# Token norms in a mixture of experts: gathered beside one expert, normed beside the next, in two fused vector passes

## The chip, the cores and the metric

One core of one Trainium2 chip runs the whole program. A core has TensorE (PE, matrix products), VectorE (DVE), ScalarE (ACT), GpSimd (POOL) and SyncE (SP), each with an in-order queue of its own, and 16 DMA engines that they share. The metric is device time of one execution in microseconds (us); lower is better.

## The reference

A decoder layer with 2048 tokens of 1024 values: a mixer, a LayerNorm, a mixture of 16 experts with two experts for a token, and a second LayerNorm. The change lies in the second half:

```python
def moe(x, ...):                       # idx, w = route(x): 2 of 16 experts a token
    ...
    h = jax.nn.silu(xb @ w_gate[e]) * (xb @ w_up[e])      # w_gate, w_up: 1024 x 512
    return h @ w_down[e]                                   # w_down: 512 x 1024
...
x = layer_norm(ALPHA * x + moe(x, ...), ln2_g[l], ln2_b[l])

def layer_norm(x, g, b):
    mu = jnp.mean(x); var = jnp.mean(jnp.square(x - mu))   # over a token's 1024 values
    return (x - mu) * lax.rsqrt(var + LN_EPS) * g + b
```

## The kernel before

The function `moe_phase` treats the experts in 16 steps, s = 0 to 15, in an order chosen on the chip. A step has room for CAPS[s] tokens: 264 in steps 8 and 9, 256 from step 10 on (two chunks of 128 rows). A product in float32 is made of three passes over high and low halves, so every operand is split on the chip: ScalarE copies the high half, VectorE subtracts to get the low half.

**The first product** of a step (`gemm1`, line 62, tiles `ph`) has four quarters j. A quarter takes two weight tiles, gate and up, of 128x1024; each is loaded by SyncE into `raw` (four buffers), copied by ScalarE (L1569) and completed by VectorE (L1570, tile `w`, four buffers). When both results are there, ScalarE applies silu (L1575) and VectorE multiplies (L1576, tile `sl`); that product of the activations is what the change hangs the norms on. ScalarE and VectorE then split it into `h` (L1584, L1585). After quarters 1 and 2 the halves of the down weights are split as well (L1546, L1547, 128x2048).

**The second product** (`gemm2`, L1621, tiles `py`) multiplies `h` with the down weights. For a chunk of 128 rows, TensorE first takes the quarters 0 to 2 of both halves and then quarter 3. ScalarE evicts to `z` (L1636, two buffers), and GpSimd adds it to the sum `zd` in DRAM by an indirect scatter (L1658). Between these products TensorE transposes the next step's tokens (L1484), whose halves go to `xt` (L1486). TensorE's order is written by hand; the other engines' orders come from a scheduler that goes by a simulated time line.

**The next steps' tokens** come by `fetch`: SyncE loads the slot table (`tab`, L1461), VectorE makes indices of it (`tb`, `ig`, `io`, L1463 to L1467), and GpSimd gathers the rows (`xg`, L1471). SyncE issues the table's load behind the weight loads, each of which stands for a `raw` buffer that a split on VectorE releases.

**The norm of finished tokens.** The tokens are put into an order (`fin`) by the last of their experts, and after step s - 1 a known number of blocks of 128 tokens is final (READY). Beside step s the function `tokens` norms those blocks: 2, 1, 2, 1, 2, 2, 2 and 4 in steps 8 to 15. For each, GpSimd gathers the rows from `zd` (`zt`, L1524), VectorE takes the statistics of the two halves (L1527), aggregates them (L1501) and adds epsilon (L1503), GpSimd raises to -1/2 (L1504), VectorE computes the shift (L1506), ScalarE scales and shifts (L1509), GpSimd multiplies with g (L1510), VectorE adds b (L1511), and GpSimd scatters the result to the output (L1532). The gather can't be issued before the last scatter of step s - 1 has landed in `zd`. Tiles `zt` and `o` have two buffers.

The last step's own 256 tokens are added to a gathered residual and normed in `gemm2` itself (L1633 to L1663, L1514, L1515). A loop for overflowing slots and one for tokens whose norm must be repeated follow; they run zero times here.

Of the kernel before, what the change touches and what calls it, by code (L numbers as in the profile page):

```python
# [11 lines left out]
F32 = mybir.dt.float32  # L12
# [5 lines left out]
OP = mybir.AluOpType  # L18
# [4 lines left out]
D = 1024  # L23
# [5 lines left out]
ALPHA = 2.0 ** 0.25  # L29
# [988 lines left out]
NE = 16  # L1018
# [408 lines left out]
def moe_phase(c):  # L1427
    nc, tc, a = c.nc, c.tc, c.a
    v = nc.vector
    CM = CAPS[0]  # L1430
    NCH = (CM + 127) // 128
    with ExitStack() as es:
# [20 lines left out]
        def indirect(idx):  # L1453
            return bass.IndirectOffsetOnAxis(ap=idx, axis=0)
# [60 lines left out]
                v.scalar_tensor_tensor(o[:r, vs], o[:r, vs], rs[:r], b2[:r, vs], op0=OP.mult, op1=OP.add)  # L1515
            return o

        def tokens(row=None, idx=None):

            z = yp.tile([128, D], F32, name="zt")  # L1520
            if idx is None:
                nc.gpsimd.dma_start(z, c.z[ds(row, 128), :])
            else:
                nc.gpsimd.indirect_dma_start(out=z, out_offset=None, in_=c.z[:, :], in_offset=indirect(idx))  # L1524
            st = sm.tile([128, 2, 6], F32, name="st")
            for hf in range(2):
                v.bn_stats(st[:, hf], z[:, hf * 512:(hf + 1) * 512])  # L1527
            o = normed(z, st, 128)
            if idx is None:
                nc.gpsimd.dma_start(out[ds(row, 128), :], o)  # L1530
            else:
                nc.gpsimd.indirect_dma_start(out=out, out_offset=indirect(idx), in_=o, in_offset=None)  # L1532

        def after(order, *instructions):
            for i in instructions:
                order.enter_context(tc.issue_after(i.ins))
# [13 lines left out]
        def gemm1(f, e, C, first=False, late=False):  # L1550
            xh = lambda k: f["xt"][k // 4][:, 0, k % 4]
            xl = lambda k: f["xt"][k // 4][:, 1, k % 4]
            h = ht[:, :, :C], ht[:, :, 384:384 + C]

            off = stacked(C)
            full = C // 128 * 128 if off else C
            for j in range(4):
                ps = []
                for w in (wg, wu):
                    raw = w1p.tile([128, KC, 128], F32, name="raw1")  # L1560
                    load = nc.sync.dma_start(raw, w[ds(e, 1), :, j * 128:(j + 1) * 128].rearrange("o (k p) f -> p (o k) f", p=128))
                    if j == 1 and first:

                        hold(c, load, f["gather"])
                    t = w1p.tile([128, 2, KC, 128], F32R, name="w1")
                    with ExitStack() as order:
                        if j and first:
                            after(order, *f["last"])
                        nc.scalar.activation(t[:, 0], raw, AF.Copy)  # L1569
                        v.tensor_tensor(out=t[:, 1], in0=raw, in1=f32(t[:, 0]), op=OP.subtract)  # L1570
                    pg = ps_h.tile([128, 512], F32, name="ph")[:, :C]
                    matmul3(nc, pg, lambda k: t[:, 0, k], lambda k: t[:, 1, k], xh, xl, KC)
                    ps.append(pg)
                sl = hp.tile([128, CM], F32, name="sl", bufs=2)[:, :C]
                silu = nc.scalar.activation(sl, ps[0], AF.Silu)  # L1575
                mul = v.tensor_tensor(out=sl, in0=sl, in1=ps[1], op=OP.mult)  # L1576
                f.setdefault("mul", mul)

                with ExitStack() as order:
                    after(order, silu, mul)  # L1580
                    for part in THEN[j]:
                        if part < 2:
                            f["w"] = f.get("w", []) + [down(e, part)]
                nc.scalar.activation(h[0][:, j], sl, AF.Copy)  # L1584
                low = v.tensor_tensor(out=h[1][:, j, :full], in0=sl[:, :full], in1=f32(h[0][:, j, :full]), op=OP.subtract)  # L1585
                if off:
                    v.tensor_tensor(out=ht[:, j, full + off:C + off], in0=sl[:, full:], in1=f32(h[0][:, j, full:]), op=OP.subtract)
                if 2 in THEN[j] and late:
                    with ExitStack() as order:
                        after(order, low)  # L1590
                        residual(f, C)
            f["h"] = h
# [91 lines left out]
        with tc.manual_schedule(engines={mybir.EngineType.PE}):  # L1684
            r = plan_slots(c, pl, ps_y)

            big = lambda n: yp.tile([128, D], F32, name="zt")[:, :n * NE].rearrange("p (n e) -> p n e", e=NE)
            order_, over = plan_order(c, pl, ps_y, r, big), plan_over(c, pl, r, big)
            f = start(0)
            early = sm.tile([128, 128], BF16, name="early")  # L1690
# [2 lines left out]
            for step in transposes(f, CAPS[0]):  # L1693
                step()
                keep_warm(c, ps_y, WARM5)
            for s in range(NE):
                late = last = s == NE - 1
                nxt = start(s + 1) if 0 < s < NE - 1 else None
                gemm1(f, E[s], CAPS[s], s == 0, late)
                with ExitStack() as order:  # L1700
# [5 lines left out]
                    else:  # L1706
# [2 lines left out]
                            next(over, None)  # L1709
                        for _ in range(0 if s < 3 else 2 if s == 5 else 1):  # L1710
                            next(order_, None)
                for b in range(READY[s - 2] if s > 1 else 0, READY[s - 1] if s else 0):

                    tokens(idx=c.fin[:, b, 0:1])
                work = gemm2(f, E[s], CAPS[s], late, last)
                if nxt:
                    steps = transposes(nxt, CAPS[s + 1])
# [12 lines left out]
            run(gemm2(f, e, 128))  # L1730
        n = nc.values_load(c.nagain[0:1, 0:1], min_val=0, max_val=S // 128)
        with tc.For_i(0, n, 1) as i:
            tokens(row=i * 128)


def fill_tables(c, pad, part):
# [53 lines left out]
```

## Time and profile before

| | |
|---|---|
| Time, median of 3 runs | 1772.26 us (1771.97 to 1775.58) |
| The profiled execution's own time | 1779.3 us |
| Its span, first to last instruction | 1777.8 us |
| Mean granted TensorE clock | 0.941 |
| TensorE busy | 1546.0 us, 87% |
| VectorE busy | 1200.3 us, 68% |
| ScalarE busy | 773.7 us, 44% |
| GpSimd busy | 641.2 us, 36% |
| DMA | 260.77 MB, mean 147 GB/s |
| First products of steps 8 to 15 begin at | 1341.83, 1405.78, 1454.07, 1504.33, 1552.33, 1600.41, 1649.20 and 1694.70 us |

The shares are means over phases with different limits: the mixer ends near 950 us, and the steps 8 to 15, the ones with norms, take the last 436 us. For these the list of waits and the engines' timelines say more than the shares. In such rows a name such as `zt<-zd,fin` reads "tile zt, made from zd and fin", L1527 is line 1527 of the kernel before, and a wait is put down to the event that ended it.

### The profile page before, as it was taken

Reading aid. Unit: us, or ns where it says so; the run is one execution under the profiler, and the core shown is the slowest. Engines: PE = TensorE matmul, PEld = TensorE weight load, DVE = VectorE, ACT = ScalarE, POOL = GpSimd, SP = SyncE. Lnnn points to the kernel's source line nnn. Section 1 sums busy time; section 2 is a strip of 40 time slices with the busy share of each in tenths; the row PEclk is TensorE's granted clock in tenths of the full one; section 3 lists DMA queues with packets and bytes.
Section 4 is the critical chain, followed back from the end, with each engine's and each line's share of the span. In section 5 each row is a group of like instructions: output and inputs, shape, how many; then the busy total and the mean of one; then the engine's idle time right before and its main releaser. Section 6 shows DMA issues by size and latency. Waiting matters only on the chain. (4 is left out here: it accounts for less than half of the span.)

```text
span 1777.8 us, 28720 instructions
## 1 busy us (share of the span) xinstructions
PE 1546.0 (87%) x10277; PEld 1383.0 (78%) x10277; DVE 1200.3 (68%) x2900; ACT 773.7 (44%) x1605; POOL 641.2 (36%) x814
## 2 busy tenths in 40 slices
PE   8899999888889988889995999999995986877881
PEld 7899999877888887767773999988884876777770
DVE  5788888985888888578885566555542555565643
ACT  4567676762211123233322545555543453444430
POOL 3233343555555544123232221111233424233334
PEclk9999999999999999989997999999998998988895
DMA  9422222432123213444324987777674866778642
GB/s 274 127 90 90 90 90 90 149 102 79 55 63 97 63 42 95 162 154 172 125 96 138 308 209 198 196 193 192 180 186 101 225 191 195 206 210 234 182 118 100
DMA packets 241166, 260.77 MB, mean 147 GB/s; under 512 B 25301, under 2 KB 190358, under 8 KB 241020
## 3 DMA queue, kind: packets, MB, share of 16 engines
q1 hardware_dynamic: 213680, 182.11, 33.5%
q0 software_dynamic: 22224, 71.84, 15.4%
q10 hardware_dynamic: 5116, 4.94, 0.9%
q8 instruction: 83, 1.36, 0.3%
q14 instruction: 63, 0.52, 0.1%
HBM read 189.97 MB, written 70.60 MB: 147 GB/s over the span
## 5 line engine op out<-in xcount | busy, mean ns | idle before, releaser
L62 PE MATMUL ph<-xt,w 128*128 128x256 f32 (+8 forms) x3072 | 416.1, 298 | 80.9 <-DVE w L1570 76.2
L62 PEld LDWEIGHTS ph<-xt,w 128*128 128x128 f32 x3072 | 412.3, 196 | 86.0 <-DVE w L1570 78.5
L62 PE MATMUL pj<-xt,w 128*128 128x256 f32 x2016 | 294.7, 291 | 11.4 <-DVE xt L138 3.9
L62 PEld LDWEIGHTS pj<-xt,w 128*128 128x128 f32 x2016 | 264.3, 194 | 17.1 <-DVE xt L138 5.4
L1621 PE MATMUL py<-w,h 128*128 128x512 f32 (+8 forms) x936 | 244.6, 407 | 3.8 <-ACT z L1636 2.0
L1570 DVE TENSOR_TENSOR w<-raw,w 128x1024 fp32r<-128x1024 f32 x128 | 161.0, 1272 | 69.3 <-ACT w L1569 68.9
L1621 PEld LDWEIGHTS py<-w,h 128*128 128x128 f32 (+8 forms) x936 | 160.6, 180 | 50.0 <-issue 3.4
L62 PE MATMUL py<-w,xt 128*128 128x512 f32 x672 | 172.4, 405 | 0.0
L1569 ACT ACTIVATE w<-raw 128x1024 fp32r<-128x1024 f32 x128 | 132.7, 1053 | 59.8 <-PE ph L62 41.6
L1658 POOL DMA_INDIRECT zd<-z,io x40 | 69.7, 1743 | 236.5 <-ACT xt L1486 140.0
L62 PEld LDWEIGHTS py<-w,xt 128*128 128x128 f32 x672 | 122.8, 191 | 27.1 <-issue 4.6
L1486 DVE TENSOR_TENSOR xt<-tr,xt 128x512 fp32r<-128x512 f32 (+8 forms) x84 | 49.4, 595 | 69.2 <-ACT xt L1486 69.1
L62 PE MATMUL pj<-w,xt 128*128 128x512 f32 x336 | 88.4, 402 | 0.0
L338 POOL TENSOR_SCALAR prob<-prob,den 128x128 f32<-128x128 f32 x128 | 46.2, 380 | 108.3 <-ACT prob L381 57.8
L793 DVE TENSOR_TENSOR qb<-qq,F 64x256 f32<-64x256 f32 x112 | 83.5, 745 | 2.0
L1471 POOL DMA_INDIRECT xg<-x1d,ig x42 | 45.4, 1080 | 86.8 <-issue 33.9
L1547 DVE TENSOR_TENSOR w<-raw,w 128x2048 fp32r<-128x2048 f32 x32 | 75.2, 2350 | 0.7 <-ACT w L1546 0.7
L1527 DVE BATCH_NORM_STATS2 st<-zt 128x6 f32<-128x512 f32 x32 | 20.5, 681 | 80.1 <-DMA zt<-zd,fin 80.1
L1235 POOL DMA_INDIRECT T<-row,dst x32 | 34.5, 1077 | 111.0 <-DVE dst L1233 92.2
L811 DVE COPY_PREDICATED A<-mask,pl 128x512 f32<-128x512 uint8 x56 | 50.0, 893 | 32.1 <-PE pl L809 31.1
L1486 ACT ACTIVATE xt<-tr 128x512 fp32r<-128x512 f32 (+8 forms) x84 | 43.7, 521 | 62.0 <-PE tr L1484 62.0
L1636 ACT ACTIVATE z<-py,tb 128x512 f32<-128x512 f32 (+1 forms) x62 | 42.6, 688 | 62.3 <-PE py L1621 60.8
(366 smaller groups left out, 2937.3 us busy)
## 6 DMA issues: line engine op xcount, KB each, us to landing
raw<-in_w_gate SPq DMA_DIRECT2D x64, 512.0 KB, 6.9
raw<-in_w_up SPq DMA_DIRECT2D x64, 512.0 KB, 6.6
raw<-in_w_down SPq DMA_DIRECT2D x32, 1024.0 KB, 8.5
xd<-xt SPq DMA_DIRECT2D x32, 512.0 KB, 6.6
xr<-in_x SPq DMA_DIRECT2D x14, 1024.0 KB, 6.3
xt<-xd POOLq DMA_DIRECT2D x20, 512.0 KB, 5.0
raw<-mixT SPq DMA_DIRECT2D x16, 512.0 KB, 4.6
x1d<-x SPq DMA_DIRECT2D x16, 512.0 KB, 2.6
```

Source lines behind the costliest of these rows:

```text
L62: nc.tensor.matmul(ps, lhsT=a, rhs=b, start=i == 0, stop=i == len(steps) - 1)
L338: nc.gpsimd.tensor_scalar(prob[:, h], prob[:, h], den[:, h:h + 1], 1.0, op0=OP.mult, op1=OP.mult)
L793: nc.vector.tensor_tensor(out=qb[l][rw, :, :, o].rearrange("p a c (n i) -> p (a c) n i", i=h), in0=sec(Qv), in1=sec(Fv), op=OP.mult)
L811: c.level = nc.vector.copy_predicated(A.rearrange("p c h (n u i) -> p (c h n) u i", u=2, i=h)[:, :, 1], mask[:, l].rearrange("p m (n i) -> ...
L1471: gather = nc.gpsimd.indirect_dma_start(out=X[:r, n], out_offset=None, in_=c.x1[:, :], in_offset=indirect(ig[:r, n:n + 1]))
L1486: f["last"] = nc.scalar.activation(hi, pt, AF.Copy), v.tensor_tensor(out=lo, in0=pt, in1=f32(hi), op=OP.subtract)
L1547: v.tensor_tensor(out=t[:, 1], in0=raw, in1=f32(t[:, 0]), op=OP.subtract)
L1569: nc.scalar.activation(t[:, 0], raw, AF.Copy)
L1570: v.tensor_tensor(out=t[:, 1], in0=raw, in1=f32(t[:, 0]), op=OP.subtract)
L1621: nc.tensor.matmul(pys[hf][:m], lhsT=lhs, rhs=rhs, start=k == 0 and i == 0, stop=k == 3 and i == len(steps[k]) - 1)
L1636: nc.scalar.activation(z[:r, hs], py[:r], AF.Copy, scale=weight)
L1658: nc.gpsimd.indirect_dma_start(out=c.z[:, :], out_offset=at, in_=z[:r], in_offset=None, bounds_check=S - 1, oob_is_err=False, compute_op=O ...
```

## The change

`tokens` is cut into three parts. `bring` gathers a block; `scale` takes the statistics and the power; `write` norms in two fused VectorE passes (subtract the mean and multiply with g; multiply with the power and add b) and scatters the result. A block brought beside step s is normed beside step s + 1. `zt` gets a third buffer. The two parts of a norm are ordered behind the products of the activations (`f["muls"]`, one a quarter): `scale` of the n-th block behind quarter n's, `write` behind quarter n + 1's, at most 3. In the last step the four blocks that are left are brought and normed too, behind the last quarters.

```diff
-        def tokens(row=None, idx=None):
+        def bring(row=None, idx=None):
-            z = yp.tile([128, D], F32, name="zt")
+            z = yp.tile([128, D], F32, name="zt", bufs=3)
...
+            return dict(z=z, row=row, idx=idx)
+        def scale(t):
             st = sm.tile([128, 2, 6], F32, name="st")
             for hf in range(2):
-                v.bn_stats(st[:, hf], z[:, hf * 512:(hf + 1) * 512])
-            o = normed(z, st, 128)
...
+                v.bn_stats(st[:, hf], t["z"][:, hf * 512:(hf + 1) * 512])
+            t["mv"] = sm.tile([128, 2], F32, name="mv")
+            v.bn_aggr(t["mv"], st)
+            t["rs"] = sm.tile([128, 1], F32, name="rs")
+            v.tensor_scalar(t["rs"], t["mv"][:, 1:2], 1e-5 / ALPHA ** 2, None, op0=OP.add)
+            nc.gpsimd.tensor_tensor(out=t["rs"], in0=t["rs"], in1=mh, op=OP.pow)
+        def write(t):
+            o = yp.tile([128, D], F32, name="o")
+            v.scalar_tensor_tensor(o, t["z"], t["mv"][:, 0:1], g2, op0=OP.subtract, op1=OP.mult)
+            v.scalar_tensor_tensor(o, o, t["rs"], b2, op0=OP.mult, op1=OP.add)
...
                 f.setdefault("mul", mul)
+                f["muls"] = f.get("muls", []) + [mul]
...
-                for b in range(READY[s - 2] if s > 1 else 0, READY[s - 1] if s else 0):
-                    tokens(idx=c.fin[:, b, 0:1])
+                def norm(n, t):
+                    for k, part in enumerate((scale, write)):
+                        with ExitStack() as order:
+                            after(order, f["muls"][min(n + k, 3)])
+                            part(t)
+                ids = [c.fin[:, b, 0:1] for b in range(READY[s - 2] if s > 1 else 0, READY[s - 1] if s else 0)]
+                for n, t in enumerate(brought):
+                    norm(n, t)
+                brought = [bring(idx=i) for i in ids[:3]]
+                if last:
+                    for n in range(len(ids)):
+                        norm(2 + n // 2, brought[n])
+                        if n + 3 < len(ids):
+                            brought.append(bring(idx=ids[n + 3]))
```

TensorE's and SyncE's orders are the same in both kernels, apart from line numbers. On VectorE, step 14, from the first quarter's product on, before (`sl` is that product, `w` of 128x1024 a split of the first product's weights, `w` of 128x2048 one of the down weights):

```order
L1576 TENSOR_TENSOR sl<-sl,ph 128x256
L1570 TENSOR_TENSOR w_17895<-raw_17893,w_17895 128x1024
L1585 TENSOR_TENSOR h<-sl,h 128x256
L1527 BN_STATS st<-zt 128x6 x2
L1501 BN_AGGR mv<-st 128x2
L1503 TENSOR_SCALAR rs<-mv 128x1
L1506 SCALAR_TENSOR_TENSOR nm<-mv,rs 128x1
L1527 BN_STATS st<-zt 128x6 x2
L1576 TENSOR_TENSOR sl<-sl,ph 128x256
L1547 TENSOR_TENSOR w_17858<-raw_17856,w_17858 128x2048
L1570 TENSOR_TENSOR w_17935<-raw_17933,w_17935 128x1024
```

The same place in the changed kernel, up to the splits of the fourth quarter:

```order
L1590 TENSOR_TENSOR sl<-sl,ph 128x256
L1531 BN_STATS st<-zt 128x6 x2
L1584 TENSOR_TENSOR w_17841<-raw_17839,w_17841 128x1024
L1600 TENSOR_TENSOR h<-sl,h 128x256
L1533 BN_AGGR mv<-st 128x2
L1535 TENSOR_SCALAR rs<-mv 128x1
L1590 TENSOR_TENSOR sl<-sl,ph 128x256
L1561 TENSOR_TENSOR w_17804<-raw_17802,w_17804 128x2048
L1541 SCALAR_TENSOR_TENSOR o<-zt,mv,g_11350 128x1024
L1531 BN_STATS st<-zt 128x6 x2
L1584 TENSOR_TENSOR w_17881<-raw_17879,w_17881 128x1024
L1584 TENSOR_TENSOR w_17911<-raw_17909,w_17911 128x1024
```

The statistics stood for blocks gathered in the same step; now they are of blocks gathered a step before, and a fused pass and the second block's statistics stand ahead of the fourth quarter's splits. The rows go on as follows, up to the third quarter's low half `h`, which the second product reads:

```order
L1600 TENSOR_TENSOR h<-sl,h 128x256
L1542 SCALAR_TENSOR_TENSOR o<-o,rs,b_11351 128x1024
L1533 BN_AGGR mv<-st 128x2
L1590 TENSOR_TENSOR sl<-sl,ph 128x256
L1561 TENSOR_TENSOR w_17874<-raw_17872,w_17874 128x2048
L1584 TENSOR_TENSOR w_18070<-raw_18068,w_18070 128x1024
L1584 TENSOR_TENSOR w_18100<-raw_18098,w_18100 128x1024
L1535 TENSOR_SCALAR rs<-mv 128x1
L1541 SCALAR_TENSOR_TENSOR o<-zt,mv,g_11350 128x1024
L1584 TENSOR_TENSOR w_18135<-raw_18133,w_18135 128x1024
L1600 TENSOR_TENSOR h<-sl,h 128x256
```

Three fused passes in all stand between the second quarter's product and that half. The second place is VectorE at the end of step 11, where the slot table of a later step (`tab`) is read between the low halves `xt` of step 12's tokens. Before:

```order
L1486 TENSOR_TENSOR xt_16769<-tr,xt_16769 128x4x128
L1486 TENSOR_TENSOR xt_16770<-tr,xt_16770 128x4x128 x2
L1463 TENSOR_TENSOR tb<-tab 128x4
L1465 TENSOR_SCALAR ig<-tb 128x2
L1467 CAST io<-tb 128x2
L1570 TENSOR_TENSOR w_17023<-raw_17021,w_17023 128x1024
```

And in the changed kernel:

```order
L1486 TENSOR_TENSOR xt_16739<-tr,xt_16739 128x4x128 x2
L1463 TENSOR_TENSOR tb<-tab 128x4
L1465 TENSOR_SCALAR ig<-tb 128x2
L1467 CAST io<-tb 128x2
L1486 TENSOR_TENSOR xt_16740<-tr,xt_16740 128x4x128 x2
L1584 TENSOR_TENSOR w_16993<-raw_16991,w_16993 128x1024
```

Two of the four low halves now stand behind the table; in the changed kernel it is two in step 9 and one in steps 10 and 12; before, it was one in each of these. The third place is GpSimd, from the gathers of step 14's blocks on. Before:

```order
L1524 DMA zt_17998<-zd_88,fin_14987 128x1024
L1524 DMA zt_18015<-zd_88,fin_14987 128x1024
L1504 TENSOR_TENSOR rs_18005<-rs_18005,mh_11355 128x1
L1510 TENSOR_TENSOR o_18010<-o_18010,g2_11350 128x1024
L1532 DMA out_0<-o_18010,fin_14987 2048x1024
L1504 TENSOR_TENSOR rs_18022<-rs_18022,mh_11355 128x1
L1510 TENSOR_TENSOR o_18027<-o_18027,g2_11350 128x1024
L1532 DMA out_0<-o_18027,fin_14987 2048x1024
L1658 DMA zd_88<-z_18034,io_17302 2048x1024
```

And in the changed kernel:

```order
L1524 DMA zt_17968<-zd_88,fin_14987 128x1024
L1536 TENSOR_TENSOR rs_17949<-rs_17949,mh_11355 128x1
L1524 DMA zt_17970<-zd_88,fin_14987 128x1024
L1546 DMA out_0<-o_17952,fin_14987 2048x1024
L1536 TENSOR_TENSOR rs_17961<-rs_17961,mh_11355 128x1
L1546 DMA out_0<-o_17964,fin_14987 2048x1024
L1673 DMA zd_88<-z_17974,io_17254 2048x1024
```

The multiplies with g are gone, the power and the output scatter are of blocks gathered a step earlier and stand behind the first new gather, and the second gather stands behind the first power.

More of the change, by code (lines that the diff above doesn't have):

```diff
@@ L1524, in tokens @@
                 nc.gpsimd.indirect_dma_start(out=z, out_offset=None, in_=c.z[:, :], in_offset=indirect(idx))
+            return dict(z=z, row=row, idx=idx)
+        def scale(t):
             st = sm.tile([128, 2, 6], F32, name="st")
             for hf in range(2):
-                v.bn_stats(st[:, hf], z[:, hf * 512:(hf + 1) * 512])
-            o = normed(z, st, 128)
-            if idx is None:
-                nc.gpsimd.dma_start(out[ds(row, 128), :], o)
+                v.bn_stats(st[:, hf], t["z"][:, hf * 512:(hf + 1) * 512])
[8 more added lines that the diff above has]
+            v.scalar_tensor_tensor(o, o, t["rs"], b2, op0=OP.mult, op1=OP.add)
+            if t["idx"] is None:
+                nc.gpsimd.dma_start(out[ds(t["row"], 128), :], o)
             else:
-                nc.gpsimd.indirect_dma_start(out=out, out_offset=indirect(idx), in_=o, in_offset=None)
+                nc.gpsimd.indirect_dma_start(out=out, out_offset=indirect(t["idx"]), in_=o, in_offset=None)
         def after(order, *instructions):
@@ L1685, in moe_phase @@
             r = plan_slots(c, pl, ps_y)
-            big = lambda n: yp.tile([128, D], F32, name="zt")[:, :n * NE].rearrange("p (n e) -> p n e", e=NE)
+            big = lambda n: yp.tile([128, D], F32, name="zt", bufs=3)[:, :n * NE].rearrange("p (n e) -> p n e", e=NE)
             order_, over = plan_order(c, pl, ps_y, r, big), plan_over(c, pl, r, big)
@@ L1695, in moe_phase @@
                 keep_warm(c, ps_y, WARM5)
+            brought = []
             for s in range(NE):
@@ L1732, in moe_phase @@
         with tc.For_i(0, n, 1) as i:
-            tokens(row=i * 128)
+            t = bring(row=i * 128)
+            scale(t)
+            write(t)
 def fill_tables(c, pad, part):
```

## The prediction

> **What bounds the kernel now.** I read the list of waits first, because the engine shares (PE busy 87% of the span) say nothing about one stage. Columns: engine, line waited at, releaser, then total us, times, longest.
>
> ```profile
> DVE st L1527 <- DMA zt<-zd,fin: 80.1, 9, 13.3
> PE ph L62 <- DVE w L1570: 76.2, 10, 17.0
> DVE tb L1463 <- DMA tab<-T: 72.2, 14, 7.9
> POOL zt L1524 <- DMA zd<-z,io: 37.6, 7, 7.8
> ```
>
> The first two have nearly the same size: VectorE stands 80.1 us before the statistics of a gathered token block, and TensorE stands 76.2 us for weight splits that VectorE makes. The timeline of VectorE in step 10 shows that the two are one stall (start, duration, engine, line, operation; in brackets the idle time ahead and its releaser):
>
> ```profile
> 1463.59 0.41 DVE L1585 TENSOR_TENSOR h<-sl,h 128x256 fp32r<-128x256 f32 x1
> 1475.52 1.29 DVE L1527 BATCH_NORM_STATS2 st<-zt 128x6 f32<-128x512 f32 x2 [11.51 <-DMA zt<-zd,fin]
> ...
> 1478.01 0.42 DVE L1576 TENSOR_TENSOR sl<-sl,ph 128x256 f32<-128x256 f32 x1
> ```
>
> VectorE is in order: 11.51 us before the statistics, and the splits for the last quarter of the first product stand behind them. TensorE's timeline has this once in each of the steps 8 to 15:
>
> ```profile
> 1379.73 8.65 PE L62 MATMUL ph<-xt,w 128*128 128x264 f32 x46 [17.00 <-DVE w L1570]
> 1430.22 7.43 PE L62 MATMUL ph<-xt,w 128*128 128x264 f32 x46 [6.59 <-DVE w L1570]
> 1483.97 7.63 PE L62 MATMUL ph<-xt,w 128*128 128x256 f32 x46 [11.78 <-DVE w L1570]
> 1532.13 7.47 PE L62 MATMUL ph<-xt,w 128*128 128x256 f32 x46 [6.64 <-DVE w L1570]
> 1552.33 17.43 PE L62 MATMUL ph<-xt,w 128*128 128x256 f32 x146
> 1580.47 7.22 PE L62 MATMUL ph<-xt,w 128*128 128x256 f32 x46 [10.72 <-DVE w L1570]
> 1600.41 17.43 PE L62 MATMUL ph<-xt,w 128*128 128x256 f32 x146
> 1624.68 7.30 PE L62 MATMUL ph<-xt,w 128*128 128x256 f32 x46 [6.84 <-DVE w L1570]
> 1673.78 8.19 PE L62 MATMUL ph<-xt,w 128*128 128x256 f32 x46 [7.18 <-DVE w L1570]
> 1694.70 17.43 PE L62 MATMUL ph<-xt,w 128*128 128x256 f32 x146
> 1720.08 7.36 PE L62 MATMUL ph<-xt,w 128*128 128x256 f32 x46 [7.95 <-DVE w L1570]
> ```
>
> The eight waits are 17.00 + 6.59 + 11.78 + 6.64 + 10.72 + 6.84 + 7.18 + 7.95 = 74.7 us. TensorE is what the rest of these steps waits for, so they lie on the path.
>
> **The change, part by part.**
>
> *The wait goes.* A block is gathered beside one step and read beside the next, over 20 us later, while a gather lands 4.2 to 6.3 us after its issue:
>
> ```profile
> DMA to landing us min/median/max: 4.2/5.1/6.3
> ```
>
> No statistics then wait for their gather in steps 9 to 14. TensorE's and SyncE's orders stay as they are. On GpSimd the power and the output scatters now stand behind the new gathers, and the second gather of steps 13 to 15 stands for a buffer that a fused pass releases; behind these are a step's own scatters, which come half a step later. **Gain 74.7 us.**
>
> *The slow matmuls behind each wait go.* At full speed 146 matmuls of 256 columns take 17.43 us, 0.1194 each, so 46 take 5.49, and 5.66 with 264 columns (steps 8 and 9). The 46 behind the waits took 8.65, 7.43, 7.63, 7.47, 7.22, 7.30, 8.19 and 7.36: together 17.0 us more. The granted clock agrees: in the busy times by stretch (last three numbers of a row: granted clock, DMA share, GB/s; the first with an x is TensorE) it is 1.00 in step 1, where TensorE never waits, and 0.86 in step 10.
>
> ```profile
> 1026.00:1072.00 46.00, 46.00 (x283) 41.95 (x282) 28.62 (x51) 22.58 (x31) 11.88 (x9) 1.00 0.78 196
> 1454.00:1504.00 50.00, 37.76 (x256) 35.10 (x256) 26.95 (x39) 22.80 (x30) 20.51 (x13) 0.86 0.69 197
> 1600.00:1649.00 49.00, 40.02 (x259) 36.14 (x258) 27.27 (x38) 21.33 (x28) 17.95 (x13) 0.90 0.80 221
> ```
>
> A short wait costs clock too. In step 13, TensorE stood 2.02 us and the next 12 matmuls took 4.61 us, against 3.04 for 12 a moment later: 1.6 more.
>
> ```profile
> 1641.53 4.61 PE L1621 MATMUL py<-w,h 128*128 128x512 f32 x12 [2.02 <-ACT z L1636]
> ...
> 1646.32 3.04 PE L1621 MATMUL py<-w,h 128*128 128x512 f32 x12
> ```
>
> I therefore add 1.6 us to every new wait of some 2 us or more. The Trainium skill (TensorE: Matmul & The Clock Gate, What's actually happening) says that the clock falls only after an idle window of about 3.4 us. By that rule the new waits below would cost no clock, and the sum would be some 10 us better; the row of 2.02 us speaks against it.
>
> **Gain 17.0 us.** The 2.02 us wait itself is for an evicted block whose scatter came late, because GpSimd was busy with the norms' multiplies and output scatters; those multiplies go: **gain 3.6 us**, nothing if the scatter stays late.
>
> *What VectorE gets.* The norm leaves ScalarE (one activation) and GpSimd (one multiply per block), and VectorE's one add becomes two fused passes. Nothing waits for ScalarE or GpSimd here except the chain removed above, so I count no gain for them. A fused pass of 832 columns takes 1.085 us; for 1024 I take 1.25 from start to start, between that and its length scaled by columns (1.34).
>
> ```profile
> L1514 DVE SCALAR_TENSOR_TENSOR o<-z,mv,g x2: 1085/1085/1085, 1753.3 to 1762.3; 128x832 f32<-128x832 f32 x2
> ```
>
> For the rest, start to start, from step 9: product 0.34, down weights' split 2.20, two splits 2.27, low half 0.34.
>
> ```profile
> 1432.77 0.42 DVE L1576 TENSOR_TENSOR sl<-sl,ph 128x264 f32<-128x264 f32 x1
> 1433.11 2.28 DVE L1547 TENSOR_TENSOR w<-raw,w 128x2048 fp32r<-128x2048 f32 x1
> 1435.31 2.35 DVE L1570 TENSOR_TENSOR w<-raw,w 128x1024 fp32r<-128x1024 f32 x2
> 1437.58 0.41 DVE L1585 TENSOR_TENSOR h<-sl,h 128x256 fp32r<-128x256 f32 x1
> ```
>
> A first product lasts 192 x 0.1194 = 22.9 us, a quarter 5.73. By the fixed order, VectorE does the following from the second quarter's product (at 11.6) to the third quarter's low half, with two blocks: 0.34 + 2.20 + pass 1.25 + statistics 1.3 + 2.27 + 0.34 + pass 1.25 + aggregate 0.2 + 0.34 + 2.20 + 2.27 + add 0.1 + pass 1.25 + split 1.14 + 0.34 = 16.8, so it ends at 28.4. The second product needs that half after 8 matmuls of 0.25, at 22.9 + 2.05 = 24.95: 3.4 us late. With one block the list is 2.85 shorter: 0.6 late. Two blocks are normed beside steps 9, 11, 13 and 14, one beside 10 and 12. **Loss 4 x (3.4 + 1.6) + 2 x 0.6 = 21.2 us.** Bounds: 0, if TensorE's own small waits give the room, and twice that.
>
> *The table wait comes to the front.* VectorE also stands for the slot table, in its order among the transposes' low halves. The table landed 12.5 and 10.4 us after the end of the split that releases its issue (steps 10 and 12):
>
> ```profile
> 1493.19 1.22 DVE L1570 TENSOR_TENSOR w<-raw,w 128x1024 fp32r<-128x1024 f32 x1
> 1506.85 0.16 DVE L1463 TENSOR_TENSOR tb<-tab 128x4 f32<-128x4 f32 x1 [6.02 <-DMA tab<-T]
> 1507.23 0.68 DVE L1486 TENSOR_TENSOR xt<-tr,xt 128x512 fp32r<-128x512 f32 x1
> ...
> 1588.82 1.23 DVE L1570 TENSOR_TENSOR w<-raw,w 128x1024 fp32r<-128x1024 f32 x1
> 1600.42 0.16 DVE L1463 TENSOR_TENSOR tb<-tab 128x4 f32<-128x4 f32 x1 [2.05 <-DMA tab<-T]
> ```
>
> By the list, that split ends at 27.0 with one block and 29.9 with two; the table then is there at 38.5 and 41.4, and the low halves behind it take 1.0 (one) or 1.65 (two). TensorE needs them 1.4 us into the next step. A step without waits is 1600.41 - 1552.33 - 10.72 - 1.73 = 35.6 us, so the need is at 37.6 with one block and at 42.0 with two. New waits: step 10 to 11 and 12 to 13 1.9 each (one low half behind the table; + 1.6 each), 11 to 12 1.0 (two behind it): 8.0 us. Of these, 3.5 are there now, at the start of step 11 (1.95 and 1.6 of clock):
>
> ```profile
> 1507.97 17.52 PE L62 MATMUL ph<-xt,w 128*128 128x256 f32 x133 [1.95 <-DVE xt L1486]
> ```
>
> **Loss 4.5 us**, bounds 0 and 11.
>
> *The last step.* TensorE's first product now ends at 1720.08 + 7.36 = 1727.4, and from there to the end of the span (1777.8) are 50.4 us; VectorE starts the last step's own norm here:
>
> ```profile
> 1753.35 1.08 DVE L1514 SCALAR_TENSOR_TENSOR o<-z,mv,g 128x832 f32<-128x832 f32 x1 [3.48 <-DMA out<-o,fin]
> ```
>
> Behind it VectorE will have nine passes (11.3), two pairs of statistics (2.6), four evictions (2.8), their statistics (2.5), small ones (1.2) and the pass at L1514 (1.1), 21.5 in all, with some 3 us of waits for the last two gathers, whose buffers come free late; from L1514 on, 24.5 us remain as now. That is 49 instead of 50.4: **gain 1.4 us**, bounds -6 and +6.
>
> **The sum.** 74.7 + 17.0 + 3.6 - 21.2 - 4.5 + 1.4 = 71.0 us. The profiled execution took 1779.3 us, so 1708.3. It lies 7.0 us above the median of the runs, 1772.26; I carry that over: **1701 us**.
>
> **The rivals.**
>
> *Nothing new waits.* The losses of 21.2 and 4.5 do not come: 1701 - 26 = 1675. For it: in step 1 TensorE was busy 46.00 of 46.00 us, with 28.6 us of VectorE beside it. Against it: 16.8 us of VectorE work in 13.4. Chance 0.12.
>
> *The clock holds through waits of 2 to 3 us.* Six additions of 1.6 fall away: 1701 - 10 = 1691. This is what the Trainium skill's page on the clock gate would give. Against it stands the row of 2.02 us. Chance 0.15.
>
> *The transfers bind.* In step 13 the DMA engines were busy 0.80 of 49 us, 39 us of work; the others have about 35 (step 10: 0.69 of 50). My steps 8 to 14 sum to about 290 us, 41 each, a share of 0.85. The highest share at which TensorE never waited is 0.78 (1026 to 1072). If that is the limit, a step takes 35/0.78 = 45 us, seven of them 314: 24 more, 1725, and up to 1745 if the weights come in an order that starves the splits. Against it: in bursts the engines are busy throughout. Chance 0.22.
>
> *Slower.* GpSimd raises the variance to the power -1/2 behind the new gathers in its queue, and these stand until the last scatter has landed:
>
> ```profile
> 1472.44 0.97 POOL L1524 DMA_INDIRECT zt<-zd,fin  x1 [0.30 <-issue]
> ```
>
> Step 10 began at 1454.1, so the gathers were out at 19.3 us; the second pass asks for the power at about 20 (11.6 + the list to there). Each us later stops VectorE, all splits and TensorE behind it, in seven steps. It eats the 71 us when the gathers come 10 us later than now, and ends at 1772 + 91 - 71 = 1792 when they come 13 later. Nothing in the trace moves them so far; GpSimd gets less to do. Chance 0.04. That the order doesn't do what it says, and some statistics still wait for a gather of the same step, is left with 0.02, near 1770.
>
> **How the numbers follow.** The forecast has 0.45. The range leaves out most of the cases beyond 1725 and the few below 1674: 1674 to 1730. A measurement tells 0.2%, 3.5 us, from no change. Faster: 0.45 + 0.12 + 0.15 + 0.22 = 0.94; the same 0.02; slower 0.04.
>
> **What would show it.** Right: the wait of the statistics for their gathers falls from 80.1 to under 10 us (the last step's), no wait of TensorE above 5 us in steps 9 to 14, and those that remain stand before the second product and 1.4 us into steps 11 to 13. Wrong: waits of ScalarE for weights (transfers bind), waits of the second pass for GpSimd (the slower case), or first products of 22.9 us with whole steps of 36 (nothing new waits). If the clock rows stay at 0.9 with short waits, the clock term was mis-sized.

## The result and the profile after

The changed kernel took 1725.77 us (median of 4 runs, 1723.19 to 1729.72) against 1773.92 us for the kernel before (4 runs, 1771.97 to 1778.47): a ratio of 0.9727, 95% interval 0.9699 to 0.9755. A later series on another chip gave 1722.40 us (6 runs) against 1772.71, ratio 0.9711 (0.9685 to 0.9736). So it gains 48 to 50 us; the prediction had 1701 us, a gain of 71.

First the waits of the changed kernel's profiled execution (1723.19 us), in the columns of before. Line numbers have moved: the statistics are now L1531, the weights' split L1584, the low half of the activations L1600, the second product L1636.

```profile
DVE tb L1463 <- DMA tab<-T: 83.4, 14, 10.4
PE py L1636 <- DVE h L1600: 17.7, 9, 3.4
PE ph L62 <- DVE w L1584: 3.3, 7, 0.7
DVE o L1542 <- POOL rs L1536: 2.8, 2, 2.5
DVE st L1531 <- DMA zt<-zd,fin: 2.5, 1, 2.5
```

The pair that made the stall is gone: the statistics' 80.1 us are 2.5, TensorE's 76.2 us for weight splits are 3.3. Two waits have grown: TensorE's for the activations' low half, and VectorE's for the slot table (72.2 before). Where they fall is seen in TensorE's timeline from step 8 on:

```profile
1358.94 0.51 PE L62 MATMUL ph<-xt,w 128*128 128x264 f32 x2 [3.33 <-ACT w L1583]
...
1392.44 0.59 PE L1484 MATMUL tr<-ident,xg 8*128 8x8 f32 x4 [4.69 <-DVE xt L1486]
1392.96 5.29 PE L1636 MATMUL py<-w,h 128*8 128x512 f32 x12
...
1426.66 0.50 PE L1636 MATMUL py<-w,h 128*128 128x512 f32 x1 [2.67 <-DVE h L1600]
1469.99 0.76 PE L1636 MATMUL py<-w,h 128*128 128x512 f32 x1 [3.42 <-DVE h L1600]
1500.53 5.68 PE L62 MATMUL ph<-xt,w 128*128 128x256 f32 x46 [0.39 <-DVE w L1584]
1510.80 0.63 PE L1636 MATMUL py<-w,h 128*128 128x512 f32 x1 [2.75 <-DVE h L1600]
1549.29 0.50 PE L1636 MATMUL py<-w,h 128*128 128x512 f32 x1 [0.86 <-DVE h L1600]
1564.90 17.52 PE L62 MATMUL ph<-xt,w 128*128 128x256 f32 x133 [2.78 <-DVE xt L1486]
1593.09 0.80 PE L1636 MATMUL py<-w,h 128*128 128x512 f32 x1 [2.72 <-DVE h L1600]
1633.82 0.74 PE L1636 MATMUL py<-w,h 128*128 128x512 f32 x1 [2.72 <-DVE h L1600]
...
1682.68 8.48 PE L1636 MATMUL py<-w,h 128*128 128x512 f32 x24 [4.50 <-DVE z L1648]
```

The eight waits of 6.59 to 17.00 us have become one of 2.7 us before the second product in each step with two normed blocks (9, 11, 13, 14), 0.86 us in step 12 with one, 3.42 in step 10, two for the next step's tokens (`xt`, 4.69 and 2.78 us), one of 3.33 us for a weight copy in step 8 and one of 4.50 us in the last step. The busy times by stretch (columns as before) show the granted clock nearly restored, 0.96 to 1.00 in steps 10 to 12 against 0.86 in step 10 before:

```profile
1441.00:1482.00 41.00, 37.46 (x256) 34.27 (x255) 25.23 (x34) 20.66 (x28) 15.07 (x9) 0.96 0.84 239
1482.00:1523.00 41.00, 37.86 (x258) 34.66 (x257) 26.32 (x36) 19.32 (x26) 10.24 (x9) 0.96 0.86 243
1523.00:1560.00 37.00, 36.14 (x259) 33.39 (x258) 23.86 (x32) 19.32 (x26) 15.80 (x8) 1.00 0.92 263
```

Lengths of the steps in us, between the starts of their first products (the last to the end of the span); the third and fourth columns are of two runs below, e9 and e7:

| step | before | changed kernel | the same, second trace | norm and table moved |
|---|---|---|---|---|
| 7 | 49.5 | 48.4 | 49.0 | 44.8 |
| 8 | 64.0 | 54.2 | 51.5 | 47.0 |
| 9 | 48.3 | 43.5 | 44.9 | 39.8 |
| 10 | 50.3 | 41.2 | 37.1 | 35.6 |
| 11 | 48.0 | 40.8 | 45.2 | 35.6 |
| 12 | 48.1 | 36.9 | 41.7 | 35.6 |
| 13 | 48.8 | 45.3 | 46.8 | 35.6 |
| 14 | 45.5 | 40.8 | 40.8 | 35.6 |
| 15 | 83.1 | 75.2 | 74.3 | 77.9 |

### The profile page after: what moved, and what is told of

It is laid out like the page before. It is cut to its first block, busy times and chain, and to the rows that moved or that the text cites. A ratio compares the mean times of both kernels' runs of the same rounds, so it can differ in the third digit from the quotient of the medians.

```text
span 1721.7 us, 28673 instructions
## 1 busy us (share of the span) xinstructions
PE 1544.5 (90%) x10277; PEld 1377.6 (80%) x10277; DVE 1199.9 (70%) x2900; ACT 755.7 (44%) x1589; POOL 600.5 (35%) x798
## 5 line engine op out<-in xcount | busy, mean ns | idle before, releaser
L62 PE MATMUL ph<-xt,w 128*128 128x256 f32 (+8 forms) x3072 | 402.0, 292 | 10.0 <-ACT w L1583 3.8
L62 PEld LDWEIGHTS ph<-xt,w 128*128 128x128 f32 x3072 | 398.7, 190 | 14.7 <-DVE w L1584 5.0
L62 PE MATMUL pj<-xt,w 128*128 128x256 f32 x2016 | 293.8, 290 | 13.1 <-DVE xt L138 3.9
L62 PEld LDWEIGHTS pj<-xt,w 128*128 128x128 f32 x2016 | 262.6, 193 | 19.4 <-DVE xt L138 5.3
L1636 PE MATMUL py<-w,h 128*128 128x512 f32 (+8 forms) x936 | 253.1, 416 | 23.4 <-DVE h L1600 17.7
L1636 PEld LDWEIGHTS py<-w,h 128*128 128x128 f32 (+8 forms) x936 | 165.7, 185 | 72.7 <-DVE h L1600 21.6
L1584 DVE TENSOR_TENSOR w<-raw,w 128x1024 fp32r<-128x1024 f32 x128 | 153.7, 1218 | 67.8 <-ACT w L1583 67.6
L1673 POOL DMA_INDIRECT zd<-z,io x40 | 65.9, 1646 | 262.6 <-ACT xt L1486 147.0
L1486 DVE TENSOR_TENSOR xt<-tr,xt 128x512 fp32r<-128x512 f32 (+8 forms) x84 | 49.4, 595 | 71.2 <-ACT xt L1486 71.0
L62 PEld LDWEIGHTS pj<-w,xt 128*128 128x128 f32 x336 | 60.7, 191 | 10.6
```

Source lines behind the costliest of these rows:

```text
L62: nc.tensor.matmul(ps, lhsT=a, rhs=b, start=i == 0, stop=i == len(steps) - 1)
L1486: f["last"] = nc.scalar.activation(hi, pt, AF.Copy), v.tensor_tensor(out=lo, in0=pt, in1=f32(hi), op=OP.subtract)
L1636: nc.tensor.matmul(pys[hf][:m], lhsT=lhs, rhs=rhs, start=k == 0 and i == 0, stop=k == 3 and i == len(steps[k]) - 1)
L1673: nc.gpsimd.indirect_dma_start(out=c.z[:, :], out_offset=at, in_=z[:r], in_offset=None, bounds_check=S - 1, oob_is_err=False, compute_op=O ...
```

## The experiments

Two questions were put to the chip: which part of the change makes the gain, and where the 21 to 23 us went that the prediction had beyond it. "Before" was timed in each series on the same chip: 1774.77 us (e1 to e4), 1773.59 (e5 to e8), 1772.71 (e9 to e11).

**e1: the distance undone.** Passes and places as changed, but a block is normed beside the step that gathers it.

```
+brought = [bring(idx=i) for i in ids[:3]]
+if not last:
+    for n, t in enumerate(brought):
+        norm(n, t)
-for n, t in enumerate(brought):
-    norm(n, t)
-brought = [bring(idx=i) for i in ids[:3]]
```

> The fused passes stay, fixed behind the products as in the changed kernel, but each block is gathered and normed beside the same step; only the gather's distance from its use is undone (the last step keeps its own order). Theory (the gain is the gather's wait): the statistics of steps 8 to 14 stand for their gathers again, 60 to 80 us in all, TensorE waits for weight splits 5 to 12 us a step, and the time goes back to 1765 to 1800 us (before 1774). Rival (the gain is the norm's new form, off ScalarE and GpSimd): it stays at 1726 to 1740 us.

Measured: 1762.60 us, ratio 0.9935 (0.9909 to 0.9960). Its waits:

```profile
DVE st L1531 <- DMA zt<-zd,fin: 53.7, 8, 12.5
...
PE ph L62 <- DVE w L1584: 47.4, 7, 13.7
```

Both stalls are back, a little under the theory's 60 to 80 us, and the time too is a little under its 1765 us. Of the gain, 11 to 12 us survive.

**e2: the distance alone, with the old norm.**

```
 def norm(n, t):
-    for k, part in enumerate((scale, write)):
-        with ExitStack() as order:
-            after(order, f["muls"][min(n + k, 3)])
-            part(t)
+    st = sm.tile([128, 2, 6], F32, name="st")
+    for hf in range(2):
+        v.bn_stats(st[:, hf], t["z"][:, hf * 512:(hf + 1) * 512])
+    o = normed(t["z"], st, 128)
+    nc.gpsimd.indirect_dma_start(out=out, out_offset=indirect(t["idx"]), in_=o, in_offset=None)
```

> The other half alone: blocks are gathered one step ahead, as in the changed kernel, but normed as before (ScalarE's activation, GpSimd's multiply, VectorE's add) and not fixed behind the products. Theory (the distance is the gain, the norm's form is worth little): 1715 to 1740 us, the statistics' wait for gathers stays below 10 us. Rival (the fused passes carry the gain): 1750 us or more, with VectorE's add waiting for GpSimd's multiply in steps 9 to 14.

**e3: the distance and the fused passes, without the fixed places.**

```
 def norm(n, t):
-    for k, part in enumerate((scale, write)):
-        with ExitStack() as order:
-            after(order, f["muls"][min(n + k, 3)])
-            part(t)
+    scale(t)
+    write(t)
```

> The changed kernel without the fixing of the passes behind the activations' products; the scheduler places them. Theory (the waits before the second product come from the sum of VectorE's work in the first product, wherever it stands): within 10 us of 1726. Rival (the fixed places spread the work and are needed): 10 to 40 us slower, with longer waits of TensorE for weight splits in the first product. A third way: it is faster by 5 us or more, since the places were badly chosen.

Measured: e2 1769.03 us, ratio 0.9985 (0.9965 to 1.0006), and e3 1765.90 us, 0.9967 (0.9945 to 0.9989). My theory fell in both. The interval of e2 includes no change at all. In e2 the rival gave the number but not the cause, since it is not an add that waits for a multiply; in e3 its longer waits for weight splits came. The waits of e2, then of e3:

```profile
DVE st L1732 <- DMA zt<-zd,fin: 78.7, 8, 12.9
PE ph L62 <- DVE w L1584: 73.8, 10, 17.1
```

```profile
DVE st L1531 <- DMA zt<-zd,fin: 75.7, 9, 14.3
...
PE ph L62 <- DVE w L1584: 71.9, 10, 16.9
```

The stall of before stands there whole, although the code reads each block a step later. GpSimd's and VectorE's timelines of e3 in step 10 (from 1444.90 us on) show how:

```profile
1462.39 1.01 POOL L1524 DMA_INDIRECT zt<-zd,fin  x1 [2.73 <-DMA zd<-z,io]
```

```profile
1467.11 1.29 DVE L1531 BATCH_NORM_STATS2 st<-zt 128x6 f32<-128x512 f32 x2 [11.82 <-DMA zt<-zd,fin]
```

The statistics stand in the same step as their gather, 4.7 us behind its issue, and VectorE waits 11.82 us for it. VectorE's order comes from the scheduler. I take it that the scheduler draws an instruction forward to where its simulated time line has the data, while on the chip the data are not there yet; the rows show only the order that came out. Code that asks for the result one expert later did not keep the two apart; the places behind the products do. So the gain needs distance and places together: distance without places gives 3 to 9 us, places without distance 11 to 12, both 48 to 50. Whether the fused form is needed as well is not shown, because distance and places with the old norm were not run.

**e4: the norms of the blocks gathered beside steps 8 to 14 left out.**

```
-for n, t in enumerate(brought):
-    norm(n, t)
-brought = [bring(idx=i) for i in ids[:3]]
+brought = [bring(idx=i) for i in ids[:3]] if last else []
```

> Leaves out the gather, the norm and the output scatter of the 12 blocks that are normed beside steps 9 to 14 (the last step's four are kept), so their rows are not written. It bounds what the remaining norms cost the path. Theory (VectorE's list still sets the second product's start and the clock behind it): the waits before the second product of steps 9 to 14 go (2.67, 3.42, 2.75, 0.86, 2.72, 2.72 us, 15.1 in all, and about 10 us of half clock behind them), so 1726 - 25 = about 1700 us, with the waits for the slot table still there. Rival (the transfers set the steps' length): the same steps shorten by 10% or more also where no such wait stood (step 12, 36.9 us), below 1685 us. Rival (nothing of the norm is left on the path): 1720 us or more.

**e8: gather and scatter kept, arithmetic left out.**

```
+def move(t):
+    nc.gpsimd.indirect_dma_start(out=out, out_offset=indirect(t["idx"]), in_=t["z"], in_offset=None)
 for n, t in enumerate(brought):
-    norm(n, t)
+    move(t)
```

> Leaves out the norm's arithmetic for the 12 blocks of steps 9 to 14: each block is gathered and scattered as in the changed kernel, with no statistics and no passes, so these rows hold unnormed values. The transfers are the same, VectorE and GpSimd are free of the norm. Theory (what is left of the norm's cost is VectorE's time, not the transfers): the same time as the run that leaves the blocks out altogether, within 5 us, about 1700 us. Rival (the transfers of the blocks cost): 10 us or more above that run, with the DMA share above 0.85 in steps 9 to 14.

Measured: e4 1678.77 us (0.9467, 0.9427 to 0.9507), e8 1693.75 us (0.9552, 0.9530 to 0.9573). So what is left of the norms costs 44 to 47 us, nearly twice what my theory had, and the blocks' transfers alone are 15 of it. (Some 8 to 9 of the 44 to 47 lie in the last step, which has two blocks fewer to norm in e4: 66.2 us there against 75.2 and 74.3; e8 has 71.2.) In numbers that is the rival of bound transfers, in both runs. The sign of e4's rival fails, for step 12 lasts 37.4 us in e4 against 36.9 in the changed kernel's first trace. The sign of e8's rival comes, a DMA share above 0.85 in most of these steps, but step 10 of e8 has the highest share, 1.00, and lasts 35.6 us without a wait of TensorE. The place of the waits says something else. VectorE's reads of the slot table in steps 11 and 12, e4 and then e8:

```profile
1501.09 0.16 DVE L1463 TENSOR_TENSOR tb<-tab 128x4 f32<-128x4 f32 x1 [6.50 <-DMA tab<-T]
1538.88 0.17 DVE L1463 TENSOR_TENSOR tb<-tab 128x4 f32<-128x4 f32 x1 [6.86 <-DMA tab<-T]
```

```profile
1508.39 0.16 DVE L1463 TENSOR_TENSOR tb<-tab 128x4 f32<-128x4 f32 x1 [9.36 <-DMA tab<-T]
1551.65 0.16 DVE L1463 TENSOR_TENSOR tb<-tab 128x4 f32<-128x4 f32 x1 [10.38 <-DMA tab<-T]
```

With the blocks' transfers beside it VectorE stands 2.9 and 3.5 us longer for the table, and TensorE behind it waits 4.43 and 5.17 us for `xt` instead of 1.55 and 1.92. Counted from the end of the split that releases the table's issue, the five tables of steps 8 to 12 come after 12.5 to 13.7 us in e4 and after 13.9 to 16.2 in e8. The next runs test directly what the table costs.

**e5: the norm behind the splits.** The statistics go behind the first quarter's product, both passes behind the last low half of the activations, so beside the second product.

```
-low = v.tensor_tensor(out=h[1][:, j, :full], ...)
+low = f["low"] = v.tensor_tensor(out=h[1][:, j, :full], ...)
...
-after(order, f["muls"][min(n + k, 3)])
+after(order, f["muls"][min(n + k, 3)] if last else f["low"] if k else f["muls"][0])
```

> The changed kernel with VectorE's norm moved behind the splits: the statistics of all blocks behind the first quarter's product, both passes behind the fourth quarter's low half, so beside the second product (steps 9 to 14; the last step as in the changed kernel). Theory (the passes in front of the second product's first needed half make TensorE's waits there): those waits (15.1 us in steps 9 to 14) fall below 3 us, the half clock behind them (about 2 us each) goes, 1726 - 20 to 25 = 1701 to 1706 us. Rival (what is taken from there comes back as later low halves of the next step's tokens, since the passes now stand in front of these): the waits for the tokens 1.4 us into the step grow from 2.8 us by 2 to 3 us a step, and the time stays within 6 us of 1726.

**e6: the table read behind the low halves**, in the fetches issued from step 7 on.

```
-v.tensor_tensor(out=tb, in0=tab[:, 0], in1=tab[:, 1], op=OP.min)
+with ExitStack() as order:
+    after(order, *behind)
+    v.tensor_tensor(out=tb, in0=tab[:, 0], in1=tab[:, 1], op=OP.min)
...
-nxt = start(s + 1) if 0 < s < NE - 1 else None
+nxt = start(s + 1, f["last"] if s >= 7 else ()) if 0 < s < NE - 1 else None
```

> The changed kernel with VectorE's read of the slot table of the next step moved behind the current step's last low half of transposed tokens, so that no low half stands behind the table. Theory: the two waits of TensorE for tokens 1.4 us into a step (4.69 us in step 8's end, 2.78 at the start of step 13) and the half clock behind them (about 2 us each) go: 8 to 11 us faster, 1715 to 1718 us. Rival (the table read late makes the gathers of the step after next late): TensorE waits for transposes' input instead and the time is the same or longer.

**e7: both moves.**

> Both moves of the two runs beside it (norm behind the splits, table behind the last low half). Theory (they are separate waits): the gains add, 1726 - 30 to 35 = 1691 to 1696 us. Rival (the transfers then bind): the DMA share rises above 0.90 and the gains do not add, 1700 to 1710 us.

Measured: e5 1705.49 us (0.9614, 0.9592 to 0.9636), e6 1697.34 us (0.9578, 0.9555 to 0.9601), e7 1677.80 us (0.9445, 0.9420 to 0.9470). Beside the two medians of the changed kernel, the passes in front of the second product cost 17 to 20 us (19.5 from e6 to e7), as expected: e5 has no wait for the low half left in steps 9 to 14. TensorE's waits for tokens stay in e5 (6.09 us at the end of step 8, 3.96 to 5.00 into steps 11 to 13), longer than in the first trace, as e5's rival had it; but the time is the theory's. The table costs 25 to 28 us (27.7 from e5 to e7), about three times what I expected of e6. The gains add: 45 to 48 for both.

The traces give a somewhat smaller figure for the table. In steps 8 to 14 VectorE's order in e6 is that of the changed kernel but for the three instructions on the table, so the edit does only what it says. But the medians of the changed kernel and of e6 come from different chips, and ahead of step 7, where the edit does nothing, the profiled executions already differ: step 7 begins at 1284.5 us in e6, at 1295.4 and 1290.2 in the two traces of the changed kernel. Counted from the start of step 7 the table costs 19.4 and 24.4 us beside e6, and 26.1 from e5 to e7.

e7 is as fast as e4, which leaves these norms out, but that does not make them free. In steps 10 to 14 they cost e7 nothing; its last step takes 77.9 us against 66.2 in e4. What makes up for it is that e4 still has the table in the way: its steps 7, 8 and 11 to 13 are 1.8 to 4.2 us longer each. TensorE's first product of step 12 and the stretches of steps 11 to 14 in e7:

```profile
1494.31 22.88 PE L62 MATMUL ph<-xt,w 128*128 128x256 f32 x192
```

```profile
1458.00:1494.00 36.00, 36.00 (x259) 33.66 (x258) 26.95 (x37) 19.21 (x26) 9.43 (x8) 1.00 0.99 279
1494.00:1529.00 35.00, 35.00 (x255) 32.79 (x255) 23.13 (x31) 18.97 (x26) 13.66 (x9) 1.00 0.95 286
1529.00:1565.00 36.00, 36.00 (x259) 33.65 (x258) 27.07 (x39) 19.32 (x26) 10.64 (x8) 1.00 0.98 279
1565.00:1601.00 36.00, 36.00 (x259) 33.62 (x258) 26.66 (x34) 19.28 (x26) 14.52 (x10) 1.00 0.99 287
```

All 192 matmuls of the first product run on in 22.88 us, TensorE is busy throughout at full clock, and the DMA engines at a share of 0.95 to 0.99. Transfers do not bind these steps.

**e9: the changed kernel again**, beside e10 and e11.

> The changed kernel itself, once more, beside the two kernels below on one chip, for comparison and for a second trace. Theory (the table read in VectorE's order costs 20 us or more with what hangs on it): the same time as before, 1718 to 1728 us, with the low halves late for TensorE at the start of step 9 (4 to 6 us), once or twice more in steps 10 to 13 (2 to 3 us), and half clock behind each. Rival (the 28 us between the changed kernel and the run with the table read moved are partly the chip's): below 1715 us here.

Measured: 1722.40 us (1715.50 to 1728.71). In this second trace the table's waits fall otherwise than in the first. TensorE, the ends of steps 8 and 10 to 12:

```profile
1386.09 0.59 PE L1484 MATMUL tr<-ident,xg 8*128 8x8 f32 x4 [7.58 <-DVE xt L1486]
...
1478.70 17.36 PE L62 MATMUL ph<-xt,w 128*128 128x256 f32 x133 [4.32 <-DVE xt L1486]
...
1522.95 22.82 PE L62 MATMUL ph<-xt,w 128*128 128x256 f32 x179 [3.40 <-DVE xt L1486]
...
1564.27 18.78 PE L62 MATMUL ph<-xt,w 128*128 128x256 f32 x133 [2.98 <-DVE xt L1486]
```

That is 18.3 us in four waits, where the first trace had 7.5 in two. The time is the theory's; the rival, below 1715 us, did not come. VectorE ahead of the third:

```profile
1506.92 1.21 DVE L1584 TENSOR_TENSOR w<-raw,w 128x1024 fp32r<-128x1024 f32 x1
...
1521.26 0.16 DVE L1463 TENSOR_TENSOR tb<-tab 128x4 f32<-128x4 f32 x1 [9.71 <-DMA tab<-T]
...
1521.62 1.28 DVE L1486 TENSOR_TENSOR xt<-tr,xt 128x512 fp32r<-128x512 f32 x2
```

The split that releases the table's issue ends at 1508.13, the table is there 13.1 us later, and the two low halves queued behind it end at 1522.90; TensorE goes on at 1522.95.

**e10: GpSimd's powers ahead of the gathers.** In the first trace's step 10 the second pass stood for a power that was queued behind the gathers (VectorE, then GpSimd):

```profile
1462.38 1.28 DVE L1542 SCALAR_TENSOR_TENSOR o<-o,rs,b 128x1024 f32<-128x1024 f32 x1 [2.47 <-POOL rs L1536]
```

```profile
1460.76 0.97 POOL L1524 DMA_INDIRECT zt<-zd,fin  x1 [0.31 <-issue]
1461.76 0.59 POOL L1536 TENSOR_TENSOR rs<-rs,mh 128x1 f32<-128x1 f32 x1
```

```
-brought = [bring(idx=i) for i in ids[:3]]
+with ExitStack() as order:
+    after(order, *[t["pow"] for t in brought if not last])
+    brought = [bring(idx=i) for i in ids[:3]]
```

> The changed kernel with the gathers of steps 8 to 14 put behind the powers of the blocks normed there on GpSimd, so that no second pass waits for a power behind a gather. As a side effect of the scheduler the table's read comes one low half earlier in two steps. Theory (step 10's second pass waited 2.47 us for a power behind two gathers, which made TensorE's wait there 3.42 instead of 0.86 us and cost 2 us of clock): 4 to 5 us faster, 1718 to 1724 us, and step 10 lasts 37 to 38 us, if no new wait for the table comes. Rival (the gathers then come late for the next step's statistics): no faster, and statistics wait for gathers above 5 us.

Measured: 1726.31 us, ratio 0.9736 (0.9708 to 0.9765), beside 0.9711 for e9. Step 10 lasts 37.8 us, as expected, but e9 has 37.1 there without the edit; and the table's earlier read made TensorE stand 6.75 us for tokens in step 11. The time is outside the theory's 1718 to 1724, and the rival's statistics that wait for gathers did not come either. The run does not tell what the power's wait is worth.

**e11: the last step's own blocks behind the low half too**, on top of e7.

```
-after(order, f["muls"][min(n + k, 3)] if last else f["low"] if k else f["muls"][0])
+after(order, f["low"] if k or n > 1 else f["muls"][0])
```

> The run with both moves (norm behind the splits, table's read behind the last low half), with the last step's own four blocks also moved behind the last low half of the activations. Theory (TensorE's 5.93 us before the last second product come from the norms of these blocks fixed ahead of it): the wait goes, 4 to 7 us faster, 1671 to 1674 us. Rival (VectorE bounds the last step, 45 us busy of 75, so its order there does not matter): within 3 us of 1678.

Measured: 1682.51 us (0.9487, 0.9467 to 0.9506), no better than e7 and 4.7 us above it, so neither the theory's time nor the rival's came. TensorE in the last step, e7 and then e11:

```profile
1632.41 5.84 PE L1638 MATMUL py<-w,h 128*128 128x512 f32 x16 [5.93 <-DVE h L1602]
```

```profile
1624.64 5.24 PE L1638 MATMUL py<-w,h 128*128 128x512 f32 x22
1632.47 5.83 PE L1638 MATMUL py<-w,h 128*128 128x512 f32 x24 [2.58 <-DVE z L1650]
```

The wait of 5.93 us is gone and the time with it is not: TensorE does not bound the last step (81.0 us in e11, 77.9 in e7). The rival's VectorE as its bound is not shown: it is busy 45 of the 81 us, and in both runs the chain that ended last goes through an output scatter of 3.6 to 3.7 us ahead of VectorE's last pass. What bounds the last step stays open.

e7 beats both kernels: 1677.80 us, 5.5% below the kernel before.

## Why the prediction was off by a third of its gain

**Where the gain comes from was right.** The gathers' wait (74.7 us of TensorE) and the half clock behind it (17.0) are gone, and so is the ScalarE wait of step 13. The signs named came too: the statistics' wait is 2.5 us, and no wait of TensorE in steps 9 to 14 is above 4.32. e1 shows that the gain hangs on the distance. The sum without new waits is checked by e7: the prediction's 1675 us for "nothing new waits" against 1677.80, and its 35.6 us for a step without waits against 35.6 in five steps. In the changed kernel that rival's mechanism did not occur, though; the new waits came.

**VectorE's list in front of the second product was right.** Forecast 3.4 us late with two blocks and 0.6 with one; the trace has 2.67 to 2.75 and 0.86. A pass takes 1.28 us, 1.20 from start to start (forecast 1.25). The term was 21.2 us; the medians give 17 to 20, and steps 9 to 14 of e6 and e7 differ by 21.1 us.

**The clock behind a short wait was right in size, though not every wait costs it.** I took 1.6 us for each wait of some 2 us or more. TensorE in step 11 of e6, and its stretches (the last three columns are granted clock, DMA share, GB/s):

```profile
1486.77 0.50 PE L1638 MATMUL py<-w,h 128*128 128x512 f32 x1 [2.76 <-DVE h L1602]
...
1487.59 3.78 PE L1638 MATMUL py<-w,h 128*128 128x512 f32 x9
```

```profile
1484.00:1488.00 4.00, 1.24 (x7) 0.92 1.06 369
1488.00:1492.00 4.00, 4.00 (x15) 0.66 1.12 338
1492.00:1496.00 4.00, 4.00 (x21) 1.00 1.11 350
```

The nine matmuls that took 2.34 us in step 12 of e6, behind a wait of 0.89 us, take 3.78 here, and the granted clock shows 0.66. (The DMA share can come out a little above 1; it is not read here.) But in step 11 of the second trace of the changed kernel the same nine matmuls run at full speed behind a wait just as long:

```profile
1506.72 0.50 PE L1636 MATMUL py<-w,h 128*128 128x512 f32 x1 [2.75 <-DVE h L1600]
...
1507.41 2.34 PE L1636 MATMUL py<-w,h 128*128 128x512 f32 x9
```

In the two traces of the changed kernel and in e6, TensorE stands twelve times for 2.44 to 2.76 us before the second product of steps 9, 11, 13 and 14. Nine of these waits cost about 1.5 to 1.6 us more up to the start of the next step, three cost nothing. What decides is not shown. The rule of the Trainium skill (TensorE: Matmul & The Clock Gate, What's actually happening), that the clock falls only after some 3.4 us of idle time, is not borne out by the wait of 2.76 us, and the rival built on it, 1691 us, falls.

**The step that failed is "The table wait comes to the front".** The mechanism was named, the size was wrong: 8.0 us in all, of which 4.5 new, with 11 as the outer bound. The runs give 25 to 28 us by the medians and 19 to 26 by the traces. Some 2.5 to 4 of these lie in step 7 (48.4, 49.0 and 47.3 us in the two traces and e5, against 45.0 and 44.8 in e6 and e7), which the kernel before paid as well, so the term's 8.0 stands against 16 to 24. Two things were missed:

- *The landing.* I took 11.5 us from the split's end to the table, the mean of two steps of before (12.5 and 10.4). These were the two earliest of five: in steps 8 to 12 of the kernel before, the table came 15.2, 14.4, 12.4, 13.5 and 10.4 us after that split, 13.2 in the mean. Ten landings in the two traces of the changed kernel (steps 8 to 12) come 10.6 to 17.3 us after it, 13.3 in the mean. Each later us falls on TensorE, because low halves are queued behind the table. Into steps 11, 12 and 13, where 1.9, 1.0 and 1.9 us were forecast, the first trace has landings of 10.9, 11.2 and 13.1 us and waits of 0, 0 and 2.78; the second has landings of 14.6, 13.1 and 13.3 and waits of 4.32, 3.40 and 2.98. As an estimate: with 13.3 us in place of 11.5, the prediction's own working has the tokens 3.7, 2.9 and 3.7 us late, which is 15 us with 1.6 of slow matmuls behind each, instead of 8.
- *Step 8.* The prediction looked at the tables of steps 10 to 12 only. At the end of step 8 TensorE waits 4.69 and 7.58 us in the two traces, with slow matmuls behind it (12 matmuls in 5.29 and 4.28 us; the same 12 take 2.92 in e6).

Crowding is not a third one. The steps became shorter, so the same bytes came in less time: the DMA share rose from 0.69 to 0.84 in step 10. And e8's later tables show that a block's gather and scatter can delay one. But in the mean the changed kernel's tables land no later than those of the kernel before.

**The rival of bound transfers came near the time, but by luck.** It gave 1725 us, and 1722 to 1726 came, but not by its mechanism: the share was 0.92 in step 12 of the changed kernel, where TensorE waits only 0.86 us, for VectorE, and 0.95 to 0.99 in steps 11 to 14 of e7, with TensorE never waiting. The sign named for it did appear: ScalarE waits for loaded weights in steps 9 to 14, up to 1.72 us in the first trace and 2.79 in the second, where the profile before shows no such wait in these steps. It hardly reaches TensorE, whose waits for weight splits there are 0.40 us at most. The rival's limit was a misreading as well. 0.78 is not the highest share at which TensorE never waited in the profile before; step 0, with larger products, has 1.04:

```profile
976.00:1026.00 50.00, 50.00 (x295) 45.04 (x295) 24.56 (x34) 25.29 (x34) 9.50 (x7) 1.00 1.04 296
```

What bound, beside VectorE's passes, was one small load, on which an in-order engine stood with other work behind it. That the time lies inside the stated 1674 to 1730 us owes something to luck too: 1725 us stood there for a rival whose mechanism did not come.

**The slower rival's mechanism exists, at a fraction.** It needed the powers late in seven steps. The first trace has the one wait of 2.47 us in step 10 (TensorE waits 3.42 us there, 0.86 in step 12 with one block too); the second trace has none in step 10.

**The last step** was put 1.4 us better, from the end of the first product to the end of the span 49 us. It is 51.6 and 50.7 in the two traces, 50.4 before.

So of the 21 to 23 us that the gain falls short of the forecast, the table makes 8 to 16 (16 to 24 less the 8 forecast), the last step about 2. Part of the rest lies in waits that one trace has and the other has not: the power in step 10, and 3.33 us for ScalarE's weight copies in step 8. Which of them the median holds is not settled.

## What to carry to other kernels

When a large wait is taken from an in-order engine, list everything else on which that engine stands, in every step, with the work queued behind it; price those waits with all the landings that the trace has, not with two of them. A small load read in the midst of an engine's queue can cost more than the megabytes beside it: read it behind the work that does not need it. Where a scheduler orders an engine, asking for a result later in the code may move nothing, as in e2 and e3; a fixed place did.

## What was not expected of the hardware

The DMA engines held a share of 0.95 to 0.99 and 279 to 287 GB/s over four steps of e7 without one wait of TensorE, and 1.04 and 296 GB/s in step 0 of the kernel before. So in this kernel a share near 1 is by itself no sign that transfers bind. A load of the slot table, 128x4 values read by one VectorE instruction of 0.16 us, landed 10.6 to 17.3 us after the split that releases it. Waits of TensorE of 2.4 to 2.8 us cost 1.5 to 1.6 us of slow matmuls in nine cases of twelve and nothing in three.
